# A Hymba/PEER encoder block on one core: routing look-ups and one-hot tables divided differently between VectorE and ScalarE

## The chip, the core and the metric

The kernel runs on one core of a Trainium2 chip. The metric is the device time of one execution in microseconds, as the median of several runs; the profile comes from one further execution on the same kind of core.

## The reference, cut to what matters

One encoder layer for 512 tokens of width 1024: a condition vector gives shifts, scales and gates; attention and a gating MLP share one input projection; then comes PEER, a retrieval over 128 x 128 single-neuron experts, which takes most of the time and holds the change.

```
q  = (h @ w_q) -> (tokens, 8 heads, 2 halves, 128)
s1, s2 = q[:, :, f] . keys[:, f]           # 128 scores per half
v1, i1 = top_k(s1, 16);  v2, i2 = top_k(s2, 16)
cand   = v1[:, None] + v2[None, :]         # 16 x 16
sc, ci = top_k(cand, 16)
idx    = i1[ci // 16] * 128 + i2[ci % 16]
gates  = softmax(sc)
out    = sum_k gelu(U[idx_k] . h) * gate_k * V[idx_k]
```

## The kernel before, in words

Three of the four 128-token blocks (384 tokens) go through PEER densely: for each e of 128, `dense_a` computes gelu(U_e h) for the 128 experts of row e, the result is multiplied by a table of gates and goes through V_e. The fourth block gathers its experts' rows by indirect DMA, as work inserted into the dense loop. Float32 products are made as three exact matmuls of high and low halves (`mm3`, lines 80 to 84): a cast on ScalarE makes the high half (line 77), a subtraction on VectorE the low one (line 78). So each weight tile that TensorE uses waits for one instruction of each of the two engines.

The stages around the change:

1. Query scores (lines 668 to 689): per head and half, 24 matmuls of 512 columns, a copy `qT`, four score matmuls. The weights wq have their high and low halves in two buffers each.
2. Routing on VectorE (lines 530 to 609), in two groups of four heads for the 384 dense tokens (tag d). `route_keys` takes the top 16 of 128 scores; `route_cands` adds the pairs that can be among the best 16; `route_pick` takes the top 16 of them; `route_decode` turns a candidate's number into row and column (`rcf`) and casts the key indices to bf16 (`i12f`, line 585); `route_lookup` fetches the index of each pick. A look-up compares the wanted column with 0 to 15 (line 593), multiplies by the table, which is repeated along the innermost axis (line 595), and adds up in a tree (lines 597 and 599). The one-hot tile `oh` has two buffers, one for each of the two look-ups.
3. Meanwhile TensorE computes `dense_a` for e up to 17, as far as weights and a ring of result tiles allow.
4. Table build (lines 723 to 810): the indices and gates are transposed (`gt`), then 48 steps of 8 tokens make, for each token, the one-hot of its first index times its gate (`o1`) and of its second index (`o2`), and TensorE multiplies the two into a 128 x 128 table (`gg`, line 770). Of the 8 first-index one-hots, four are made on VectorE as compare and product (line 757) and four by a bf16 compare of four tokens together (line 751) with the gate as scale on ScalarE (line 764). All eight second-index one-hots are one f32 compare (line 753). ScalarE drains the tables (line 779). Twelve further dense tiles are spread over the 48 steps. The order of TensorE, ScalarE and VectorE in this stage is that of the program.
5. Expert loop (lines 888 to 927): `dense_a(e + 30)`, the V product of e, and from the list `fill` (lines 864 to 879) the routing of the last 128 tokens (tag g) and the 256 gathers, spaced by an estimate of cost for each entry.

Outside stage 4 the order of the instructions on each engine is planned when the program is built: an instruction goes as soon as, by the planner's own estimates, its operands are ready, earlier program lines first. Each engine then works strictly in that order.

Of the kernel before, what the change touches and what calls it, by code (L numbers as in the profile page):

```python
# [19 lines left out]
P = 128  # L20
# [6 lines left out]
K = 16  # L27
# [11 lines left out]
UT = 8  # L39
# [18 lines left out]
def tile_kernel(ctx: ExitStack, tc: tile.TileContext, a: dict, out: bass.AP):  # L58
    nc = tc.nc
    ctx.enter_context(nc.allow_low_precision("float32 products as sums of exact float32r parts"))  # L60

    def pool(st, name, side=None, space=None):
        kw = {} if space is None else {"space": space}
        return st.enter_context(tc.tile_pool(name=name, bufs=1, side=side, reuse_waits="tile", **kw))
# [23 lines left out]
    iota = const("iota_s", [P, P], a["iota"])  # L88
# [29 lines left out]
    with ExitStack() as fr:  # L118
# [120 lines left out]
        for b in range(NB):  # L239
            t = B.tile([P, D], F32, name=f"x{b}", tag=f"y{b}")  # L240
# [19 lines left out]
        with ExitStack() as s1st:  # L260
# [55 lines left out]
            for b in range(NB):  # L316
                p = pss[b]
# [225 lines left out]
    def route_keys(r, b, h, f, sv):  # L543
        tmp = r["pl"].tile([P, P], F32, name=f"tmp{r['tag']}{b}{h}{f}", tag="tmp", bufs=2)
        top16(r["v12"][:, b, h, f, :], r["i12"][:, b, h, f, :], sv, tmp)

    def route_cands(r):
        n = r["nb"] * r["nh"]
        v = r["v12"].rearrange("p b h f k -> p (b h) f k")
        cand = r["pl"].tile([P, n, NC], F32, name=f"cd{r['tag']}", tag="cand", bufs=1)  # L550
        for r0, nr, ncol, p0 in STAIR:
            sh = [P, n, nr, ncol]
            nc.vector.tensor_tensor(
                cand[:, :, p0:p0 + nr * ncol].rearrange("p b (i j) -> p b i j", j=ncol),
                v[:, :, 0, r0:r0 + nr].unsqueeze(3).to_broadcast(sh),
                v[:, :, 1, :ncol].unsqueeze(2).to_broadcast(sh), op=ALU.add)
        r["cand"] = cand
        r["ci"] = r["pl"].tile([P, n, K], U32, name=f"ci{r['tag']}", tag="ci", bufs=1)
# [6 lines left out]
    def route_decode(r):  # L565
        pl, tag, ci = r["pl"], r["tag"], r["ci"]
        n = r["nb"] * r["nh"]
        rt_ = lambda m, dt=F32: pl.tile([P, n, K], dt, name=f"{m}{tag}", tag=m, bufs=1)
        t3, t2 = rt_("t3", U32), rt_("t2", U32)
        nc.vector.tensor_single_scalar(t3, ci, 3, op=ALU.logical_shift_right)  # L570
        nc.vector.tensor_single_scalar(t2, ci, 2, op=ALU.logical_shift_right)
        row, st, u = rt_("row"), rt_("rst"), rt_("ru")
        rcf = pl.tile([P, 2, n, K], BF16, name=f"rcf{tag}", tag="rcf", bufs=1)
        nc.vector.scalar_tensor_tensor(row, t3, 5.0, t2, op0=ALU.add, op1=ALU.max)
        nc.vector.scalar_tensor_tensor(row, row, 42.0, ci, op0=ALU.add, op1=ALU.max)
        nc.vector.tensor_scalar(row, row, -48.0, 0.0, op0=ALU.add, op1=ALU.max)
        nc.vector.tensor_copy(rcf[:, 0], row)
        nc.vector.tensor_scalar(st, row, 7.0, 8.0, op0=ALU.mult, op1=ALU.add)
        nc.vector.tensor_scalar(u, row, 3.0, 24.0, op0=ALU.mult, op1=ALU.add)
        nc.vector.scalar_tensor_tensor(st, row, 15.0, st, op0=ALU.mult, op1=ALU.min)  # L580
        nc.vector.scalar_tensor_tensor(st, u, 48.0, st, op0=ALU.min, op1=ALU.min)
        nc.vector.tensor_add(st, st, row)
        nc.vector.tensor_sub(rcf[:, 1], ci, st)
        i12f = pl.tile([P, n, 2, K], BF16, name=f"i12f{tag}", tag="i12f", bufs=1)
        nc.vector.tensor_copy(i12f, r["i12"].rearrange("p b h f k -> p (b h) f k"))
        r["rcf"], r["i12f"] = rcf, i12f

    def route_lookup(r, f, dst):

        n = r["nb"] * r["nh"]  # L590
        sh = [P, n, K, K]
        oh = r["pl"].tile(sh, BF16, name=f"oh{r['tag']}{f}", tag="oh", bufs=2)
        nc.vector.tensor_tensor(oh, r["rcf"][:, f].unsqueeze(2).to_broadcast(sh),
                                jrep.unsqueeze(1).to_broadcast(sh), op=ALU.is_equal)
        nc.vector.tensor_tensor(oh, oh, r["i12f"][:, :, f, :].unsqueeze(3).to_broadcast(sh), op=ALU.mult)
        for w in (8, 4, 2):
            nc.vector.tensor_add(oh[:, :, :w, :], oh[:, :, :w, :], oh[:, :, w:2 * w, :])
        o5 = oh.rearrange("p (b h) j k -> p b h j k", h=r["nh"])
        nc.vector.tensor_add(dst, o5[:, :, :, 0, :], o5[:, :, :, 1, :])
# [13 lines left out]
    with ExitStack() as qs:  # L613
# [80 lines left out]
        r = None  # L694
        for h in range(PH):
            if h + 1 < PH:
                score(h + 1)
            while ahead < FIRST + h + 1 + (LATE if h == PH - 1 else 0):
                dense_a(ahead)
                ahead += 1  # L700
            s_sb = scores.pop(h)
            hl = h % HG
            if hl == 0:
                r = route_tiles(R, f"d{h}", ND, HG)
            for b in range(ND):
                for f in range(2):
                    route_keys(r, b, hl, f, s_sb[:, b, f, :])
            if hl == HG - 1:
                hs = slice(h - HG + 1, h + 1)
                route_cands(r)  # L710
                for b in range(ND):
                    for i in range(HG):
                        route_pick(r, b, i, sca[:, b, h - HG + 1 + i, :])
                route_decode(r)
                for f, dst in ((0, i1a), (1, i2a)):
                    route_lookup(r, f, dst[:, :, hs, :])
        route_gates(R, sca, gts, ND * PH)

    flat = lambda t, b: t.rearrange("p b h k -> p b (h k)")[:, b, :]
# [3 lines left out]
    with ExitStack() as gs:  # L723
        psq = pool(gs, "psg", space=PSUM)
        G = pool(gs, "gbuild")
        tTs = []
        for b in range(ND):
            p = psq.tile([P, 512], F32, name=f"gt{b}", tag="q", bufs=6)
            for i, src in enumerate((i1a, i2a, gts)):
                nc.tensor.transpose(p[:, i * P:(i + 1) * P], flat(src, b), ident)  # L730
            tT = G.tile([P, 3, P], F32, name=f"gT{b}")
            nc.scalar.copy(tT, p[:, :384].rearrange("p (i t) -> p i t", t=P))
            tB = G.tile([P, P], BF16, name=f"gB{b}")
            nc.scalar.copy(tB, p[:, :P])  # L734
            tTs.append((tT, tB))
        HT = UT // 2
        erep = G.tile([P, P, HT], BF16, name="erep")
        nc.vector.tensor_copy(erep, iota.unsqueeze(2).to_broadcast([P, P, HT]))
        NG = TD // UT
        GPS = TC // UT  # L740
        o1s, o1b, o2s, pgs, stages = {}, {}, {}, {}, {}

        def tok(n):
            return tTs[n * UT // P], n * UT % P

        def g_eq(n):
            (tT, tB), t0 = tok(n)
            o1b[n] = G.tile([P, P, HT], BF16, name=f"o1b{n}", tag="o1b", bufs=2)
            o2s[n] = G.tile([P, UT, P], F32, name=f"o2_{n}", tag="o2", bufs=2)
            o1s[n] = G.tile([P, UT, P], F32, name=f"o1_{n}", tag="o1", bufs=2)  # L750
            nc.vector.tensor_tensor(o1b[n], erep, tB[:, t0:t0 + HT].unsqueeze(1).to_broadcast([P, P, HT]),  # L751
                                    op=ALU.is_equal)
            nc.vector.tensor_tensor(o2s[n], iota.unsqueeze(1).to_broadcast([P, UT, P]),  # L753
                                    tT[:, 1, t0:t0 + UT].unsqueeze(2).to_broadcast([P, UT, P]), op=ALU.is_equal)
            for i in range(HT, UT):
                t = t0 + i
                nc.vector.tensor_scalar(o1s[n][:, i, :], iota, tT[:, 0, t:t + 1], tT[:, 2, t:t + 1],  # L757
                                        op0=ALU.is_equal, op1=ALU.mult)

        def g_gate(n):  # L760
            (tT, tB), t0 = tok(n)
            e = o1b.pop(n)
            for i in range(HT):
                nc.scalar.activation(o1s[n][:, i, :], e[:, :, i], AF.Copy, scale=tT[:, 2, t0 + i:t0 + i + 1])  # L764

        def g_mm(n):
            o1, o2 = o1s.pop(n), o2s.pop(n)
# [50 lines left out]
    st = {}  # L818
# [46 lines left out]
    for h in range(PH):  # L865
        for f in range(2):
            fill.append((1.6, lambda h=h, f=f: route_keys(st["r"], 0, h, f, st["sg"][:, 2 * h + f, :])))
    fill.append((1.2, lambda: route_cands(st["r"])))
    for h in range(PH):
        fill.append((1.3, lambda h=h: route_pick(st["r"], 0, h, st["sc"][:, 0, h, :])))  # L870
    fill.append((4.0, lambda: route_decode(st["r"])))
    for f in range(2):
        fill.append((5.0, lambda f=f: route_lookup(st["r"], f, st["i"][f])))
    fill.append((1.2, lambda: route_gates(st["R"], st["sc"], gtg, PH)))
    fill.append((0.3, gb_idx))
    for n in range(NS):
# [138 lines left out]
```

## Time and profile before

| | |
|---|---|
| median of 3 runs | 1567.47 us (1567.18 to 1567.62) |
| the profiled execution | 1570.06 us |
| its span, first to last instruction | 1568.3 us |
| TensorE (PE) busy | 1492.6 us, 95% |
| VectorE (DVE) busy | 1240.9 us, 79% |
| ScalarE (ACT) busy | 636.6 us, 41% |
| mean granted TensorE clock | 0.981 of full speed |

Busy shares are means over stages with different limits. Durations of matmuls are modelled to their end and overlap, so starts are compared with starts. A number in square brackets at the end of a timeline row is the engine's idle time before that instruction, with what ended it. [...] In the view of busy time by stretch, a row has the stretch, its length, the busy time and number of instructions of PE, PEld (weight loads), DVE, ACT and POOL, then the granted clock, the DMA share and GB/s. In the groups by form, a row ends with the busy time in all, the mean duration of one in ns, and the idle time before them.

### The profile page before, as it was taken

To read this page: it belongs to the slowest core of one execution; us is meant where nothing else is said; L and a number is where in the kernel's file an instruction comes from. 1 tells how busy PE (TensorE), PEld (TensorE's weight loads), DVE (VectorE), ACT (ScalarE), POOL (GpSimd) and SP (SyncE) were. 2 spreads that over 40 slices of the span, in tenths; PEclk is the share of its full clock that TensorE was granted. 3 is DMA by queue.
4 is the path that set the end of the run, shared out by engine and by line. 5 is a ranking of instruction groups with operands and counts; after the bars stand their busy time and mean duration, and the time that the engine had idled before them with its cause. 6 is when DMAs were issued, how large, how long until landed. Compare 5 with 4: busy or idle time off the path is not lost.

```text
span 1568.3 us, 21451 instructions
## 1 busy us (share of the span) xinstructions
PE 1492.6 (95%) x7675; PEld 1317.9 (84%) x7675; DVE 1240.9 (79%) x2388; ACT 636.6 (41%) x1092; POOL 397.1 (25%) x335
## 2 busy tenths in 40 slices
PE   2899999998979999999999999999999999999996
PEld 1765787887879999999999999999999999998884
DVE  6937865579989997987887878878888888886774
ACT  2533434432338997334333333333333333332343
POOL 1202100000000000002554444444544544542210
PEclk9899999999999999999999999999999999999998
DMA  9626334331325769666999999988999998987873
GB/s 366 232 79 223 130 132 148 112 104 48 101 94 159 237 211 300 218 224 220 354 351 319 321 330 328 326 318 318 336 330 314 326 325 315 333 287 230 256 237 121
DMA packets 147226, 380.71 MB, mean 243 GB/s; under 512 B 11184, under 2 KB 59840, under 8 KB 146864
## 3 DMA queue, kind: packets, MB, share of 16 engines
q1 hardware_dynamic: 103472, 221.02, 40.5%
q0 software_dynamic: 42352, 153.62, 28.7%
q10 hardware_dynamic: 1296, 4.72, 0.8%
q8 instruction: 60, 0.98, 0.2%
q14 instruction: 46, 0.38, 0.1%
HBM read 349.16 MB, written 30.15 MB: 242 GB/s over the span
## 4 chain that ended last, share of the span: by engine, by line
PE 86%; DVE 7%; DMA 3%; ACT 1%; issue 1%; POOL 0%; SPq 0%; ACTq 0%; POOLq 0%; DVEq 0%
PE out L83 11%; PE out L84 11%; PE out L82 11%; PE pa L82 11%; PE pa L84 11%; PE pa L83 11%; PE gg L770 5%; DMA wada<-w_ada 2%; PE q L82 1%; PE q L84 1%; PE q L83 1%; PE yo L82 1%; PE yo L84 1%; PE yo L83 1%; DVE macc L149 1%
## 5 line engine op out<-in xcount | busy, mean ns | idle before, releaser
L842 POOL DMA_INDIRECT gu<-peer_u,idx x128 | 181.3, 1417 | 653.6 <-DVE w17l L78 467.6
L842 POOL DMA_INDIRECT gv<-peer_v,idx x128 | 173.0, 1351 | 235.0 <-DVE accg L862 209.0
L850 DVE SCALAR_TENSOR_TENSOR scr<-gu,h2g 128x1024 bf16<-128x1024 f32 x128 | 156.5, 1222 | 24.1 <-DMA gu<-peer_u,idx 21.8
L862 DVE SCALAR_TENSOR_TENSOR accg<-gv,wg,accg 128x1024 f32<-128x1024 f32 x127 | 162.8, 1282 | 7.1 <-DMA gv<-peer_v,idx 4.6
L770 PE MATMUL gg<-o,o 128*128 128x128 f32 x768 | 96.0, 280 | 3.6 <-ACT o L764 2.0
L770 PEld LDWEIGHTS gg<-o,o 128*128 128x128 f32 x768 | 94.6, 196 | 4.1 <-ACT o L764 4.1
L908 DVE TENSOR_TENSOR a<-a,g 128x384 f32<-128x384 f32 x128 | 69.1, 550 | 6.4 <-DMA g<-gd 2.9
L764 ACT ACTIVATE o<-o1b,gT 128x128 f32<-128x128 bf16 x192 | 63.4, 405 | 13.8 <-DVE o1b L751 7.2
L518 ACT ACTIVATE a<-pa 128x384 f32<-128x384 f32 x128 | 61.7, 483 | 13.2 <-PE pa L84 13.2
L149 DVE SCALAR_TENSOR_TENSOR macc<-wada,csil,macc 128x1024 f32<-128x1024 f32 x40 | 51.2, 1280 | 9.5 <-DMA wada<-w_ada 9.1
L753 DVE TENSOR_TENSOR o<-iota_s,gT 128x1024 f32<-128x1024 f32 x48 | 58.4, 1216 | 0.3 <-PE gg L770 0.2
L757 DVE TENSOR_SCALAR o<-iota_s,gT 128x128 f32<-128x128 f32 x192 | 53.2, 339 | 0.0
L779 ACT COPY st<-gg 128x512 f32<-128x512 f32 x96 | 50.5, 581 | 0.0
L159 PE MATMUL mcol<-ident_s,macc 128*128 128x128 f32 x32 | 7.4, 391 | 26.6 <-DVE macc L146 23.1
L135 POOL DMA_DIRECT2D wada<-w_ada x32 | 17.1, 535 | 59.9 <-DVE macc L149 24.3
L159 PEld LDWEIGHTS mcol<-ident_s,macc 128*128 128x128 f32 x32 | 5.5, 201 | 28.3 <-DVE macc L146 17.9
L424 ACT ACTIVATE pe<-s,mx 128x512 f32<-128x512 f32 x16 | 11.0, 688 | 28.4 <-DVE mx L422 20.8
L684 PE MATMUL sc<-keys_s,qT 128*128 128x128 f32 x128 | 18.1, 284 | 2.8 <-ACT qT L681 2.8
L751 DVE TENSOR_TENSOR o1b<-erep,gB 128x512 bf16<-128x512 bf16 x48 | 20.0, 416 | 0.9 <-ACT gB L734 0.9
L684 PEld LDWEIGHTS sc<-keys_s,qT 128*128 128x128 f32 x128 | 15.6, 191 | 5.7 <-ACT qT L681 4.3
L531 DVE MAX8 v12d<-s 128x8 f32<-128x128 f32 x48 | 12.7, 280 | 9.4 <-ACT s L686 9.4
L431 PEld LDWEIGHTS o<-vv,pts 128*128 128x128 f32 x128 | 16.1, 192 | 2.3 <-DVE mx L422 0.8
(2789 smaller groups left out, 4952.2 us busy)
## 6 DMA issues: line engine op xcount, KB each, us to landing
gd<-st SPq DMA_DIRECT2D x12, 1984.0 KB, 7.9
g<-gd SPq DMA_DIRECT2D x31, 768.0 KB, 8.4
wada<-w_ada POOLq DMA_DIRECT2D x32, 512.0 KB, 4.7
wada<-w_ada SPq DMA_DIRECT2D x16, 512.0 KB, 10.1
x<-x SPq DMA_DIRECT2D x4, 512.0 KB, 12.4
x<-x ACTq DMA_DIRECT2D x4, 512.0 KB, 3.8
x2d<-x ACTq DMA_DIRECT2D x4, 512.0 KB, 2.8
gu<-peer_u,idx POOLq DMA_INDIRECT x128, 7.3
```

The lines of the kernel that those rows point to most:

```text
L82: nc.tensor.matmul(o, lhsT=lh, rhs=rh, start=first, stop=False)
L83: nc.tensor.matmul(o, lhsT=lh, rhs=rl, start=False, stop=False)
L84: nc.tensor.matmul(o, lhsT=ll, rhs=rh, start=False, stop=last)
L149: nc.vector.scalar_tensor_tensor(acc, w, csil[:, c:c + 1], acc, op0=ALU.mult, op1=ALU.add)
L518: nc.scalar.activation(t, p[:, :TD], AF.Gelu)
L753: nc.vector.tensor_tensor(o2s[n], iota.unsqueeze(1).to_broadcast([P, UT, P]), tT[:, 1, t0:t0 + UT].unsqueeze(2).to_broadcast([P, UT, P]), ...
L764: nc.scalar.activation(o1s[n][:, i, :], e[:, :, i], AF.Copy, scale=tT[:, 2, t0 + i:t0 + i + 1])
L770: nc.tensor.matmul(pgs[n][i // 4][:, i % 4 * P:(i % 4 + 1) * P], lhsT=o2[:, i, :], rhs=o1[:, i, :], start=True, stop=True)
L842: nc.gpsimd.indirect_dma_start(out=g, out_offset=None, in_=src, in_offset=bass.IndirectOffsetOnAxis(ap=idx[:, s:s + 1], axis=0))
L850: nc.vector.scalar_tensor_tensor(scr, g, 1.0, st["h2g"], op0=ALU.mult, op1=ALU.mult, accum_out=actg[:, n:n + 1])
L862: nc.vector.scalar_tensor_tensor(accg, g, wg[:, s:s + 1], accg, op0=ALU.mult, op1=ALU.add)
L908: nc.vector.tensor_tensor(wv3, wv3, gt[:, :, e % GE, :], op=ALU.mult)
```

## The change

In the look-ups, ScalarE casts the key indices (`route_tables`) and copies each table out into a tile `rep` of the full shape (`route_rep`), so that the product on VectorE has two dense operands. `rep` and `oh` have one buffer each: the second table is spread after the first product. In the table build, both indices of four tokens are compared in one bf16 instruction of 1024 elements. ScalarE widens the second-index half to float32, and VectorE multiplies the first-index half by the gates, 512 elements at a time. Both read every eighth bf16 element in turn, since the compare leaves two indices of four tokens next to each other. The cost estimates of the inserted entries are lowered.

```
     def route_decode(r):
...
-        nc.vector.tensor_copy(i12f, r["i12"].rearrange("p b h f k -> p (b h) f k"))
-        r["rcf"], r["i12f"] = rcf, i12f
+        r["rcf"] = rcf
+
+    def route_tables(r):
+        pl, tag = r["pl"], r["tag"]
+        n = r["nb"] * r["nh"]
         i12f = pl.tile([P, n, 2, K], BF16, name=f"i12f{tag}", tag="i12f", bufs=1)
+        nc.scalar.copy(i12f, r["i12"].rearrange("p b h f k -> p (b h) f k"))
+        r["i12f"] = i12f
+        r["rep"] = {}
+
+    def route_rep(r, f):
+        n = r["nb"] * r["nh"]
+        t = r["pl"].tile([P, n, K, K], BF16, name=f"rep{r['tag']}{f}", tag="rep", bufs=1)
+        nc.scalar.copy(t, r["i12f"][:, :, f, :].unsqueeze(3).to_broadcast([P, n, K, K]))
+        r["rep"][f] = t

     def route_lookup(r, f, dst):
...
-        oh = r["pl"].tile(sh, BF16, name=f"oh{r['tag']}{f}", tag="oh", bufs=2)
+        oh = r["pl"].tile(sh, BF16, name=f"oh{r['tag']}{f}", tag="oh", bufs=1)
...
-        nc.vector.tensor_tensor(oh, oh, r["i12f"][:, :, f, :].unsqueeze(3).to_broadcast(sh), op=ALU.mult)
+        nc.vector.tensor_tensor(oh, oh, r["rep"].pop(f), op=ALU.mult)
...
             if hl == HG - 1:
                 hs = slice(h - HG + 1, h + 1)
+                route_tables(r)
+                route_rep(r, 0)
                 route_cands(r)
...
                 route_decode(r)
-                for f, dst in ((0, i1a), (1, i2a)):
-                    route_lookup(r, f, dst[:, :, hs, :])
+                route_lookup(r, 0, i1a[:, :, hs, :])
+                route_rep(r, 1)
+                route_lookup(r, 1, i2a[:, :, hs, :])
...
-            tT = G.tile([P, 3, P], F32, name=f"gT{b}")
-            nc.scalar.copy(tT, p[:, :384].rearrange("p (i t) -> p i t", t=P))
-            tB = G.tile([P, P], BF16, name=f"gB{b}")
-            nc.scalar.copy(tB, p[:, :P])
+            gT = G.tile([P, P], F32, name=f"gT{b}")
+            nc.scalar.copy(gT, p[:, 2 * P:3 * P])
+            iB = G.tile([P, P // HT, 2, HT], BF16, name=f"iB{b}")
+            nc.scalar.copy(iB, p[:, :2 * P].rearrange("p (i u k) -> p u i k", i=2, k=HT))
...
-        erep = G.tile([P, P, HT], BF16, name="erep")
-        nc.vector.tensor_copy(erep, iota.unsqueeze(2).to_broadcast([P, P, HT]))
+        erep = G.tile([P, P, 2 * HT], BF16, name="erep")
+        nc.vector.tensor_copy(erep, iota.unsqueeze(2).to_broadcast([P, P, 2 * HT]))
...
         def g_eq(n):
...
-            nc.vector.tensor_tensor(o1b[n], erep, tB[:, t0:t0 + HT].unsqueeze(1).to_broadcast([P, P, HT]),
-                                    op=ALU.is_equal)
-            nc.vector.tensor_tensor(o2s[n], iota.unsqueeze(1).to_broadcast([P, UT, P]),
-                                    tT[:, 1, t0:t0 + UT].unsqueeze(2).to_broadcast([P, UT, P]), op=ALU.is_equal)
-            for i in range(HT, UT):
-                t = t0 + i
-                nc.vector.tensor_scalar(o1s[n][:, i, :], iota, tT[:, 0, t:t + 1], tT[:, 2, t:t + 1],
-                                        op0=ALU.is_equal, op1=ALU.mult)
+            for i in range(UT // HT):
+                ohb[n, i] = G.tile([P, P, 2, HT], BF16, name=f"oh{n}_{i}", tag="ohb", bufs=2)
+                nc.vector.tensor_tensor(
+                    ohb[n, i].rearrange("p e i k -> p e (i k)"), erep,
+                    iB[:, t0 // HT + i].rearrange("p i k -> p (i k)").unsqueeze(1).to_broadcast([P, P, 2 * HT]),
+                    op=ALU.is_equal)

         def g_gate(n):
...
-            e = o1b.pop(n)
-            for i in range(HT):
-                nc.scalar.activation(o1s[n][:, i, :], e[:, :, i], AF.Copy, scale=tT[:, 2, t0 + i:t0 + i + 1])
+            for i in range(UT // HT):
+                e = ohb.pop((n, i)).rearrange("p e i k -> p i k e")
+                ts = slice(i * HT, (i + 1) * HT)
+                nc.scalar.copy(o2s[n][:, ts, :], e[:, 1])
+                nc.vector.tensor_tensor(
+                    o1s[n][:, ts, :], e[:, 0],
+                    gT[:, t0 + i * HT:t0 + (i + 1) * HT].unsqueeze(2).to_broadcast([P, HT, P]), op=ALU.mult)
...
+    fill.append((0.0, lambda: (route_tables(st["r"]), route_rep(st["r"], 0))))
     fill.append((1.2, lambda: route_cands(st["r"])))
...
-    fill.append((4.0, lambda: route_decode(st["r"])))
-    for f in range(2):
-        fill.append((5.0, lambda f=f: route_lookup(st["r"], f, st["i"][f])))
+    fill.append((3.6, lambda: route_decode(st["r"])))
+    fill.append((4.0, lambda: route_lookup(st["r"], 0, st["i"][0])))
+    fill.append((0.0, lambda: route_rep(st["r"], 1)))
+    fill.append((4.0, lambda: route_lookup(st["r"], 1, st["i"][1])))
```

## Rows read from the trace of the kernel before

**Rows 1.** Busy time by stretch, columns as told above
```profile
345.00:420.00 75.00, 68.37 (x339) 57.63 (x339) 69.93 (x351) 21.19 (x40) 0.00 (x0) 0.98 0.22 70
475.00:1536.00 1061.00, 1061.00 (x5618) 969.37 (x5618) 874.13 (x1381) 451.48 (x771) 354.88 (x257) 1.00 0.84 290
500.00:560.00 60.00, 60.00 (x466) 60.00 (x465) 58.66 (x133) 55.02 (x142) 0.00 (x0) 1.00 0.76 229
```
**Rows 2.** Timeline, first group's look-ups: start us, us, engine, line, operation
```profile
382.62 1.21 DVE L78 TENSOR_TENSOR wq12l<-wq12r,wq12h 128x1024 fp32r<-128x1024 f32 x1
...
383.88 0.50 PE L84 MATMUL q<-h2T,wq12l 128*128 128x512 f32 x1 [2.79 <-DVE wq12l L78]
```

**Rows 3.** Timeline, tail of the routing and first steps of the table build
```profile
449.01 1.22 DVE L78 TENSOR_TENSOR u15l<-u15r,u15h 128x1024 fp32r<-128x1024 f32 x1
...
450.28 0.69 PE L84 MATMUL pa<-h2T,u15l 128*128 128x384 f32 x1 [3.22 <-DVE u15l L78]
...
456.97 1.05 ACT L77 CAST u17h<-u17r 128x1024 fp32r<-128x1024 f32 x1 [10.58 <-PE pa L83]
...
458.05 1.23 DVE L78 TENSOR_TENSOR u17l<-u17r,u17h 128x1024 fp32r<-128x1024 f32 x1 [2.88 <-ACT u17h L77]
...
465.95 0.33 PE L730 MATMUL gt<-ident_s,i2a 128*128 128x128 f32 x1 [0.54 <-DVE i2a L599]
...
467.10 0.42 DVE L751 TENSOR_TENSOR o1b<-erep,gB 128x512 bf16<-128x512 bf16 x1 [0.88 <-ACT gB L734]
```

**Rows 4.** Busy time by stretch, columns as in rows 1, after the two long waits
```profile
384.00:388.00 4.00, 4.00 (x11) 3.16 (x12) 4.00 (x19) 0.00 (x0) 0.00 (x0) 0.58 0.39 135
388.00:390.00 2.00, 2.00 (x10) 1.59 (x10) 2.00 (x15) 0.00 (x0) 0.00 (x0) 0.99 0.00 0
450.00:456.00 6.00, 5.72 (x18) 5.72 (x19) 5.17 (x8) 0.00 (x0) 0.00 (x0) 0.50 0.54 175
458.00:460.00 2.00, 2.00 (x13) 2.00 (x13) 1.95 (x3) 0.41 (x2) 0.00 (x0) 1.00 0.00 0
```

**Rows 5.** Groups by form on VectorE, 345 to 475 us: busy us, mean ns | idle
```profile
L595 DVE TENSOR_TENSOR ohd<-ohd,i12fd 128x3072 bf16<-128x3072 bf16 x4 | 13.4, 3348 | 0.0
L593 DVE TENSOR_TENSOR ohd<-rcfd,jrep 128x3072 bf16<-128x3072 bf16 x4 | 7.0, 1748 | 0.0
...
L597 DVE TENSOR_TENSOR ohd<-ohd 128x1536 bf16<-128x1536 bf16 x4 | 3.8, 946 | 0.0
...
L585 DVE CAST i12fd<-i12d 128x384 bf16<-128x384 uint32 x2 | 0.7, 352 | 0.0
```

**Rows 6.** Groups by form on ScalarE, whole span, copies of 512 and 2048 elements
```profile
L779 ACT COPY st<-gg 128x512 f32<-128x512 f32 x96 | 50.5, 581 | 0.0
...
L351 ACT COPY vv<-v 128x512 f32<-128x512 f32 x4 | 2.3, 586 | 1.1 <-PE v L350 1.1
...
L77 ACT CAST wl0h<-wl0r 128x2048 fp32r<-128x2048 f32 x1 | 1.9, 1899 | 11.5 <-DMA wl0r<-w_in 11.5
```

**Rows 7.** Chain that ended last, in the table build: start us, us, what
```profile
537.58 1.78 PE gg L770 x16
...
540.41 1.78 PE gg L770 x16
```

**Rows 8.** Timeline of the table build, one step of VectorE, and ScalarE beside it
```profile
522.62 0.42 DVE L751 TENSOR_TENSOR o1b<-erep,gB 128x512 bf16<-128x512 bf16 x1
522.96 1.22 DVE L753 TENSOR_TENSOR o<-iota_s,gT 128x1024 f32<-128x1024 f32 x1
...
523.14 1.32 ACT L764 ACTIVATE o<-o1b,gT 128x128 f32<-128x128 bf16 x4 [0.19 <-DVE o1b L751]
...
524.10 1.11 DVE L757 TENSOR_SCALAR o<-iota_s,gT 128x128 f32<-128x128 f32 x4
...
524.73 1.05 ACT L779 COPY st<-gg 128x512 f32<-128x512 f32 x2
525.12 0.42 DVE L751 TENSOR_TENSOR o1b<-erep,gB 128x512 bf16<-128x512 bf16 x1
```

More of the change, by code (lines that the diff above doesn't have):

```diff
@@ L725, in tile_kernel @@
         G = pool(gs, "gbuild")
+        HT = UT // 2
         tTs = []
@@ L730, in tile_kernel @@
                 nc.tensor.transpose(p[:, i * P:(i + 1) * P], flat(src, b), ident)
-            tT = G.tile([P, 3, P], F32, name=f"gT{b}")
-            nc.scalar.copy(tT, p[:, :384].rearrange("p (i t) -> p i t", t=P))
-            tB = G.tile([P, P], BF16, name=f"gB{b}")
-            nc.scalar.copy(tB, p[:, :P])
-            tTs.append((tT, tB))
-        HT = UT // 2
-        erep = G.tile([P, P, HT], BF16, name="erep")
-        nc.vector.tensor_copy(erep, iota.unsqueeze(2).to_broadcast([P, P, HT]))
+            gT = G.tile([P, P], F32, name=f"gT{b}")
+            nc.scalar.copy(gT, p[:, 2 * P:3 * P])
+            iB = G.tile([P, P // HT, 2, HT], BF16, name=f"iB{b}")
+            nc.scalar.copy(iB, p[:, :2 * P].rearrange("p (i u k) -> p u i k", i=2, k=HT))
+            tTs.append((gT, iB))
+        erep = G.tile([P, P, 2 * HT], BF16, name="erep")
+        nc.vector.tensor_copy(erep, iota.unsqueeze(2).to_broadcast([P, P, 2 * HT]))
         NG = TD // UT
         GPS = TC // UT
-        o1s, o1b, o2s, pgs, stages = {}, {}, {}, {}, {}
+        ohb, o1s, o2s, pgs, stages = {}, {}, {}, {}, {}
         def tok(n):
@@ L746, in g_eq @@
         def g_eq(n):
-            (tT, tB), t0 = tok(n)
-            o1b[n] = G.tile([P, P, HT], BF16, name=f"o1b{n}", tag="o1b", bufs=2)
+            (gT, iB), t0 = tok(n)
             o2s[n] = G.tile([P, UT, P], F32, name=f"o2_{n}", tag="o2", bufs=2)
             o1s[n] = G.tile([P, UT, P], F32, name=f"o1_{n}", tag="o1", bufs=2)
-            nc.vector.tensor_tensor(o1b[n], erep, tB[:, t0:t0 + HT].unsqueeze(1).to_broadcast([P, P, HT]),
-                                    op=ALU.is_equal)
-            nc.vector.tensor_tensor(o2s[n], iota.unsqueeze(1).to_broadcast([P, UT, P]),
-                                    tT[:, 1, t0:t0 + UT].unsqueeze(2).to_broadcast([P, UT, P]), op=ALU.is_equal)
-            for i in range(HT, UT):
-                t = t0 + i
-                nc.vector.tensor_scalar(o1s[n][:, i, :], iota, tT[:, 0, t:t + 1], tT[:, 2, t:t + 1],
-                                        op0=ALU.is_equal, op1=ALU.mult)
-        def g_gate(n):
-            (tT, tB), t0 = tok(n)
-            e = o1b.pop(n)
-            for i in range(HT):
-                nc.scalar.activation(o1s[n][:, i, :], e[:, :, i], AF.Copy, scale=tT[:, 2, t0 + i:t0 + i + 1])
+            for i in range(UT // HT):
[4 more added lines that the diff above has]
+                    op=ALU.is_equal)
+        def g_gate(n):
+            (gT, iB), t0 = tok(n)
+            for i in range(UT // HT):
[5 more added lines that the diff above has]
+                    gT[:, t0 + i * HT:t0 + (i + 1) * HT].unsqueeze(2).to_broadcast([P, HT, P]), op=ALU.mult)
         def g_mm(n):
```

## The prediction

> **What bounds the kernel now.** I read the stretches first, then the waits inside the one that has idle time. From 475 us to 1536 us TensorE is busy for all of 1061.00 us while VectorE has 874.13 and ScalarE 451.48 [rows 1]: no saving on another engine shortens this part, and whatever is gained before 475 us is carried to the end one for one. From 345 to 420 us, where the first four heads are routed, TensorE has 68.37 of 75 us and VectorE 69.93: there two engines hand the bound to each other.
>
> The waits say where. At 383.88 us TensorE resumes after 2.79 us without wq12l, the low half of a query weight; VectorE made it only at 382.62, behind the first two look-ups [rows 2]. In the tail of routing the same happens at 450.28: 3.22 us for u15l, made at 449.01 behind a product of 3.35 us [rows 3, 5]. That delays ScalarE's cast u17h to 456.97 and with it VectorE, idle for 2.88 us at 458.05. i2a, the end of the chain, is waited for a last 0.54 us by the transposes at 465.95. [...]
>
> **The change, part by part.** *Look-ups.* A product of 3072 elements takes 3348 ns where the table is repeated along the innermost axis; the compare of equal size takes 1748 [rows 5]. The change hands the product two dense bf16 operands, as the first tree addition has: 946 ns for 1536. On the line through 946 and 1748, 3072 elements cost 1.75 us, so each product saves 1.60. Ends: 1.75, or 3.35 if the table was not the cause. I take 1.75, as compare and addition lie on one line. The cast of the indices (352 ns alone, about 0.27 in a run of instructions) leaves VectorE too. Per group of four heads: 2 x 1.60 + 0.27 = 3.47 us of VectorE.
>
> ScalarE gets the cast (some 0.5) and two spreads of 3072 elements per group. Its copies take 581 ns for 512 and 1899 for 2048 [rows 6], so 0.858 ns each and 2.78 us a spread. Spread 0 waits for the last key index; candidates and 12 picks lie between that and its use, and ScalarE's casts queue behind it. Spread 1 can start only when product 0 has left the single buffer, and product 1 waits for it. Between them VectorE has four additions and the next compare, some 0.9 + 0.5 + 0.3 + 0.3 + 1.7 = 3.7 us, which hides 2.78 if ScalarE is free within 0.9 us. In the tail it is: it waits 10.58 us for TensorE there [rows 3]. One one-hot buffer in place of two costs no wait between engines, since all its users are on VectorE, but dependent instructions follow each other with less between them: 0 to 0.5 us per group.
>
> *First group, heads 0 to 3.* wq12l comes 3.2 to 3.5 us earlier than at 382.62, more than the 2.79 that TensorE waited: the wait goes, and with it, I take it, the half clock, 4.0 - 11 x 0.2 = 1.8 by the slices, 1.5 if 11 is rounded up. I take 2.8 + 1.5 = **4.3 us**. Ends: 0 (a ScalarE wait takes the place of this one) and 4.6.
>
> *Tail, heads 4 to 7.* u15l is behind one cast and one product: 0.27 + 1.60 = 1.87 us earlier, so 1.35 of the 3.22 stays. If so short a wait leaves the clock up, 18 matmuls at 2/13 us take 2.8 instead of 5.7: 2.9 saved, taken as 2.6. TensorE then reaches the transposes 1.9 + 2.6 = 4.5 us earlier. VectorE's chain shortens by 3.47 and the idle 2.88 (u17h follows TensorE), less 0.5: 5.9 earlier. The later one decides: **4.5 us**. Ends: 1.9 (half clock as before) and 5.9. What is late next is the last dense tile on TensorE. erep doubles to 1024 elements, 0.3 us more; the first compare waits 0.88 us for ScalarE at that point [rows 3], so it costs nothing, and 0.3 if that wait shrinks.
>
> *Table build, 48 steps of 8 tokens.* The TensorE pieces of 16 start 2.83 us apart [rows 7]. VectorE's cycle was 525.12 - 522.62 = 2.50: compare 0.34, f32 compare 1.14, four gated compares 1.02 [rows 8]. Over 500 to 560 us it is busy 58.66 of 60 and ScalarE 55.02 [rows 1], by 21.1 steps 2.78 and 2.61 a step. Now there are two bf16 compares of 1024 elements (0.34 + 512 x 0.52 ns = 0.60 each) and two products of 512 on VectorE, and two widening copies of 512 on ScalarE in place of four gates (1.32). No row has a product that reads bf16 at a distance of 8 elements. Ends: 0.61, the f32 compare's rate (1.14 for 1024), and 1.02, the four gated compares of together 512. For the copy: 0.52, half of the pair at 524.73 [rows 8], and 1.32, the four gates. I take the lower ends, since both new instructions are single long ones, and since ScalarE drains PSUM with neighbours 512 bytes apart in 581 ns, against 586 for an adjacent 512 [rows 6]. VectorE: 2.78 - 2.50 + 1.20 + 1.22 = 2.70; ScalarE: 2.61 - 1.32 + 1.05 = 2.34. Both stay under 2.83: **0 us** saved, as TensorE covers both. At the upper ends VectorE needs 3.52 and ScalarE 3.93, and the cover is gone. With two one-hot buffers of 4 tokens, the compares of a step wait for copy and product of the step before; TensorE runs one step behind with two buffers of results, so this is hidden while both engines are under 2.83. The ramp of the first three steps: -1 to +1.
>
> [...]
>
> *Last 128 tokens, inside the expert loop.* Two products get shorter and two spreads of 2048 elements (1.90 by the cast of that size) and a cast go to ScalarE; the estimates that space the inserted work fall by 2.4. All lies after 475 us, under a TensorE that never pauses, with ScalarE busy 451 of 1061 us [rows 1]: 0; up to 2 us if a spread waiting for VectorE holds the casts behind it longer than their lead. No DMA moves to another queue.
>
> **Sum.** 4.3 + 4.5 = 8.8 us. The profiled execution took 1570.06 (span 1568.3 and 1.76 around it), so 1561.3 by it; it lies 2.59 above the median of the runs, 1567.47, so the median becomes **1558.7**. Own range of this case: 1553 (both upper ends, 1 us of ramp, a little reordering) to 1565. A measurement of this kernel tells 0.2%, 3.1 us, from no change.
>
> **Rivals.**
> 1. *The build becomes bound by VectorE (slower).* Place: product and widening copy, where neighbouring elements lie 16 bytes apart. It decides as soon as a product or a copy takes more than about 0.67 us from start to start. If each element takes two slots, the product costs 2 x 0.57 = 1.14 and the copy 0.95: VectorE 2.78 - 2.50 + 1.20 + 2.28 = 3.76 a step, ScalarE 3.19. Then 48 x 0.93 = 44.6 us come on top: 1558.7 + 44.6 = 1603; at half that surcharge 1577. For: the upper ends above, and a margin of only 0.13 us a step. Against: no strided row is slow. [...] Chance 0.32.
> 2. *The tables come late (no change).* ScalarE works in order; if spread 1 stands behind a cast that waits for TensorE, as u17h does, product 1 waits and the look-ups gain nothing. At 2.78 for what saves 1.60, a spread on the path is a loss of 1.18; in both groups that is 2.36, against 2 x 1.87 = 3.74 that the first products and the casts still save: 1.4 us are left, 1566. Against: the order is planned by readiness and spread 1 is ready before u17h. Chance 0.10.
> 3. *The product does not get faster.* Then only the casts leave VectorE: 2 x 0.27, 1567. Against: the addition's row. Chance 0.03.
>
> **How the numbers follow.** The forecast has 0.55. Faster: 0.55 and the better fifth of rival 2, 0.57; slower: rival 1 and the worst of rival 2, 0.33; the same: 0.10. The range must hold rival 1 in part, or it would leave out three in ten: 1553 to 1605, with some 0.1 beyond both ends.
>
> **What would show it.** The product of 3072 at about 1750 ns and the spreads at 2.8 us beside picks; no wait of TensorE for wq12l; a wait under 1.5 us for u15l; the pieces of 16 still 2.83 us apart. Wrong: products of 512 at 1.2 us with TensorE idle in every step; product 1 waiting for the spread; new waits of TensorE for casts; or an order of VectorE's work that puts other halves behind the look-ups.

## The result, and the profile after

The changed kernel takes **1601.66 us** (median of 5 runs, 1601.43 to 1604.28); the kernel before, run beside it, 1567.62 (1567.18 to 1569.22). The ratio is 1.0219, with a 95% interval of 1.0205 to 1.0233: 2.2% slower, where 1558.7 was forecast. That is the time of the first rival, 1603. The profiled execution has a span of 1599.8 us.

Busy time by stretch of the changed kernel (stretch, its length, then PE, PEld, DVE, ACT and POOL busy with their instructions, granted clock, DMA share, GB/s), to be read against [rows 1]:

```profile
345.00:420.00 75.00, 69.81 (x350) 60.03 (x349) 68.20 (x359) 27.58 (x42) 0.00 (x0) 0.98 0.23 75
500.00:560.00 60.00, 52.73 (x366) 49.24 (x365) 56.60 (x70) 55.87 (x78) 0.00 (x0) 0.96 0.57 176
700.00:1560.00 860.00, 860.00 (x4256) 774.85 (x4255) 689.20 (x906) 306.53 (x423) 354.75 (x257) 1.00 0.86 305
```

In the table build TensorE has lost its full stretch: 52.73 of 60 us where it had 60.00. Behind the build it has no gap again, so the expert loop, with the look-ups of the last 128 tokens in it, pays and gains nothing. The loss is the build's alone, and its length shows it. This row groups the 768 build products of the changed kernel, with shortest, median and longest duration in ns and then the first and the last start:

```profile
L787 PE MATMUL gg<-o,o x768: 270/275/554, 462.3 to 639.1; 128*128 128x128 f32 x192
```

The same row of the kernel before has 468.8 to 607.2. The build lasts 176.8 us in place of 138.4: **+38.4**. It starts 6.5 us earlier, but some 2.5 of that the profile of before had lost ahead of the change: the cast wq9h, which the change does not touch, starts at 342.9 there and at 340.4 after. The routing gained about **4**. Together +34.4; the medians differ by 34.0.

The groups of the changed kernel by form, from 480 to 600 us and, for the two look-up lines, over the whole span (busy us, mean ns, idle before):

```profile
L778 ACT CAST o<-oh 128x512 f32<-128x512 bf16 x66 | 70.8, 1125 | 9.3 <-DVE oh L768 9.3
...
L779 DVE TENSOR_TENSOR o<-oh,gT 128x512 f32<-128x512 bf16 x65 | 67.2, 1078 | 0.0
...
L768 DVE TENSOR_TENSOR oh<-erep,iB 128x1024 bf16<-128x1024 bf16 x66 | 42.5, 689 | 0.0
L796 ACT COPY st<-gg 128x512 f32<-128x512 f32 x64 | 34.4, 595 | 0.0
...
L598 ACT COPY repd<-i12fd 128x3072 bf16<-128x3072 bf16 x4 | 11.0, 2752 | 5.6 <-DVE ohd L608 5.6
...
L608 DVE TENSOR_TENSOR ohd<-ohd,repd 128x3072 bf16<-128x3072 bf16 x4 | 7.0, 1748 | 0.0
```

The look-up's product went from 3348 ns [rows 5] to 1748, as forecast, and a spread takes 2752 (2.78 forecast). But the widening copy of 512 takes 1125 ns and the build's product of 512 takes 1078, while the copy out of PSUM of as many elements, 512 bytes apart, takes 595, little more than the 581 of [rows 6]. These are durations of single instructions. From start to start, which is how the prediction priced them, a pair of copies takes 2.01 to 2.05 us and a pair of products 1.95 to 1.99, as here, where the compare behind a pair starts 1.95 us after it:

```profile
525.03 2.04 DVE L779 TENSOR_TENSOR o<-oh,gT 128x512 f32<-128x512 bf16 x2
526.98 1.28 DVE L768 TENSOR_TENSOR oh<-erep,iB 128x1024 bf16<-128x1024 bf16 x2
```

One period of four steps on the chain of waits of the changed kernel (start, us, what), against the pieces of 16 that stood there before [rows 7]:

```profile
524.62 2.11 ACT o L778 x2
526.73 0.98 ACT st L796 x2
...
527.93 2.14 ACT o L778 x2
...
530.94 2.14 ACT o L778 x2
...
534.31 2.15 ACT o L778 x2
536.46 0.95 ACT u23h L77
...
537.44 1.23 DVE u23l L78
538.67 0.61 DVE oh L768
...
539.38 2.11 ACT o L778 x2
```

The chain no longer runs through TensorE. It is ScalarE, copy after copy, and once in four steps a detour: the cast u23h stands in ScalarE's order, VectorE's low half u23l follows it, the next compare stands behind u23l, and the copy of that step waits for the compare. 539.38 - 524.62 = 14.76 us for four steps, 3.69 a step; TensorE needs 2.83.

### The profile page after: what moved, and what is told of

Same layout as the page of the kernel before. It is cut to its first block, busy times and chain, and to the rows that moved or that the text cites. A ratio compares the mean times of both kernels' runs of the same rounds, so it can differ in the third digit from the quotient of the medians.

```text
span 1599.8 us, 21357 instructions
## 1 busy us (share of the span) xinstructions
PE 1504.6 (94%) x7675; PEld 1320.4 (83%) x7675; DVE 1266.9 (79%) x2289; ACT 690.6 (43%) x1005; POOL 396.6 (25%) x335
## 4 chain that ended last, share of the span: by engine, by line
PE 75%; ACT 9%; DVE 9%; DMA 3%; issue 2%; POOL 0%; SPq 0%; ACTq 0%; POOLq 0%; DVEq 0%
PE out L84 11%; PE out L83 11%; PE out L82 11%; PE pa L84 10%; PE pa L82 10%; PE pa L83 10%; ACT o L778 6%; DMA wada<-w_ada 2%; ACT st L796 2%; PE q L82 1%; PE q L83 1%; PE q L84 1%; PE yo L82 1%; PE yo L83 1%; PE yo L84 1%
## 5 line engine op out<-in xcount | busy, mean ns | idle before, releaser
L787 PE MATMUL gg<-o,o 128*128 128x128 f32 x768 | 105.4, 292 | 25.6 <-DVE o L779 25.4
L787 PEld LDWEIGHTS gg<-o,o 128*128 128x128 f32 x768 | 98.3, 201 | 36.2 <-ACT o L778 33.2
L778 ACT CAST o<-oh 128x512 f32<-128x512 bf16 x96 | 103.2, 1128 | 14.4 <-DVE oh L768 14.2
L779 DVE TENSOR_TENSOR o<-oh,gT 128x512 f32<-128x512 bf16 x96 | 99.3, 1078 | 0.0
L768 DVE TENSOR_TENSOR oh<-erep,iB 128x1024 bf16<-128x1024 bf16 x96 | 62.0, 689 | 2.5 <-ACT iB L751 2.3
L418 PE MATMUL s<-kr,qr 64*128 64x512 f32 x32 | 18.0, 641 | 0.0
```

Of the source, the lines that this page charges most:

```text
L778: nc.scalar.copy(o2s[n][:, ts, :], e[:, 1])
L779: nc.vector.tensor_tensor(o1s[n][:, ts, :], e[:, 0], gT[:, t0 + i * HT:t0 + (i + 1) * HT].unsqueeze(2).to_broadcast([P, HT, P]), op=ALU.mult)
L787: nc.tensor.matmul(pgs[n][i // 4][:, i % 4 * P:(i % 4 + 1) * P], lhsT=o2[:, i, :], rhs=o1[:, i, :], start=True, stop=True)
```

## The experiments

The first four ran on one chip (before: 1568.54, 10 runs), the next four on another (1567.82, 10 runs), the last on a third (1569.67, 9 runs). Three theories of the slow build were open: the **step** (16 bytes between neighbours makes an instruction slow), the **types** (reading bf16 and writing f32), and the **shared tile** (two engines reading one tile disturb each other).

**1. The look-ups alone.** The new routing with the table build of before.

> The kernel before with the look-ups of the change alone; the table build is that of before. Theory S (the loss is all in the build, from bf16 elements read 16 bytes apart): this part is a gain. In the trace of the changed kernel the last score copy before the tail came 3.4 us earlier and the first piece of the build 6.5 us earlier than in the trace of before, but 2.5 us of that was already there at 340 us, ahead of the change; so 1 us from the first group and some 3 from the tail: 1563.5 us, 1562 to 1565. Rival L (part of the loss is in the look-ups, hidden by a luckier start): 1566 to 1570. The prediction on record had 1558.7 for this part.

Measured: 1562.53 us (1560.66 to 1564.32), ratio 0.9964 (0.9950 to 0.9977). The look-ups gain, but about 6 us by the medians and not the 8.8 of the forecast. The waits of TensorE in the routing of this kernel, from 345 to 475 us (total us, times, longest):

```profile
PE pa L84 <- DVE u8l L78: 4.2, 1, 4.2
...
PE pa L84 <- DVE u15l L78: 1.8, 1, 1.8
```

The wait for wq12l [rows 2] is gone, and one of 4.2 us for u8l, the low half of a dense tile, is new. It is in the changed kernel too, where ScalarE's cast u8h starts at 358.0 us and VectorE makes u8l only at 393.14, behind key work; the timeline there, and the clock behind it and behind u15l (columns as in the first fence):

```profile
393.14 1.22 DVE L78 TENSOR_TENSOR u8l<-u8r,u8h 128x1024 fp32r<-128x1024 f32 x1
...
394.41 0.45 PE L84 MATMUL pa<-h2T,u8l 128*128 128x384 f32 x1 [4.24 <-DVE u8l L78]
```

```profile
396.00:398.00 2.00, 2.00 (x9) 1.81 (x8) 1.38 (x10) 0.65 (x2) 0.00 (x0) 0.50 0.57 221
446.00:450.00 4.00, 4.00 (x16) 4.00 (x15) 4.00 (x11) 0.70 (x1) 0.00 (x0) 0.57 0.76 249
```

**2. The build alone.** The routing of before with the new table build.

> The kernel before with the table build of the change alone; the look-ups are those of before. Theory S: the 48 steps take 176.8 us from the first to the last piece instead of 138.4, so 38 us on top of 1567.6: 1606 us, 1604 to 1608. Rival (the two parts help or hurt each other, e.g. ScalarE's spreads delay the build): this plus the look-ups alone would not add up to the changed kernel's 1601.7.

Measured: 1605.04 us (1603.68 to 1605.43), ratio 1.0231 (1.0216 to 1.0247). The build costs 36.5 us, the look-ups give 6.0: 30.5 together, where the full change cost 34.0 in its own comparison; the intervals, some 2 us to either side of each, allow that difference. In the profiles the parts add closely: this build lasts 176.4 us (176.8 in the full change) and starts at 466.0 us behind the old routing, 3.7 us later than behind the new one (4.3, if counted from the cast wq9h, which starts at 339.8 here and at 340.4 there).

**3. The same data, 8 bytes apart.** The whole change, with the one-hot tile laid out by list first, so that one list's neighbours are 4 elements apart instead of 8. Types, engines, counts and the shared tile stay. The constant operand of the compare is half as long and is read twice; the compare takes 682 ns in place of 689, so that plays no part.

```diff
-G.tile([P, P, 2, HT], BF16, name=f"oh{n}_{i}", tag="ohb", bufs=2)
+G.tile([P, 2, P, HT], BF16, name=f"oh{n}_{i}", tag="ohb", bufs=2)
...
-e = ohb.pop((n, i)).rearrange("p e i k -> p i k e")
+e = ohb.pop((n, i)).rearrange("p i e k -> p i k e")
```

> The changed kernel with the one-hots of four tokens laid out index by index, so that product and widening copy read every fourth bf16 element (8 bytes apart) in place of every eighth (16 bytes). Theory S (a new 16-byte stretch with every element costs a second slot): the product falls from 1078 to about 690 ns, the copy from 1128 to about 610, the pieces of 16 stand 2.84 us apart again, and the time is that of the look-ups alone, 1563.5 us (1561 to 1566). Rival M (it is the mixture of bf16 and f32 operands that is slow, not the distance): both stay at 1.1 us, the time at 1601. Rival C (VectorE and ScalarE disturb each other in the one tile that both read): the same, 1595 to 1602.

Measured: 1562.62 us (1560.09 to 1564.97), ratio 0.9957 (0.9944 to 0.9971): faster than before. Its groups by form from 480 to 600 us:

```profile
L779 DVE TENSOR_TENSOR o<-oh,gT 128x512 f32<-128x512 bf16 x86 | 55.2, 682 | 0.0
L768 DVE TENSOR_TENSOR oh<-erep,iB 128x1024 bf16<-128x1024 bf16 x84 | 54.0, 682 | 0.0
L778 ACT CAST o<-oh 128x512 f32<-128x512 bf16 x85 | 53.0, 673 | 11.5 <-DVE oh L768 10.3
```

and its pieces on TensorE's timeline:

```profile
521.24 1.95 PE L787 MATMUL gg<-o,o 128*128 128x128 f32 x16
524.08 1.95 PE L787 MATMUL gg<-o,o 128*128 128x128 f32 x16
```

The product falls from 1078 to 682 ns, the copy from 1125 to 673, and the pieces are 2.84 us apart again: the cover is back. Types and shared tile are as before, so neither can be what made the instructions slow; the step is left. The build now gains nothing against that of before (this run and experiment 1 have the same time), which is the 0 us that the forecast gave it.

**4. The price of the step.** Behind the last output of the kernel before, 96 added instructions, four of each kind: a product on VectorE and a copy on ScalarE of 512 elements, at steps from 2 to 32 bytes, bf16 and f32, the step in what is read or in what is written. Its time (1609.82, one run) says nothing.

```diff
+ph = lambda t, s: t[:, :P * s].rearrange("p (e s) -> p s e", s=s)[:, :4]
...
+for _ in range(4): nc.vector.tensor_tensor(o3(od), ph(pb, 8), gb, op=ALU.mult)
+for _ in range(4): nc.scalar.copy(o3(oa), ph(pb, 8))
```

> The kernel before with instructions added after its outputs: products with a gate and copies, each of 512 elements, four times, from bf16 at 2, 4, 8, 16 and 32 bytes from element to element and from f32 at 4, 8, 16 and 32 bytes, and writes of f32 at 8, 16 and 32 bytes. Theory S: 0.69 us on VectorE and 0.61 on ScalarE up to 8 bytes; 1.08 and 1.13 from 16 bytes on, for f32 as for bf16, and no more at 32. If it grows with the distance, 32 bytes cost more than 16; if it counts elements and not bytes, f32 at 32 bytes (8 elements) is the first slow one. Rival M: all bf16 cases are slow and no f32 case is. Writes: no theory has a number from a row; 0.69 if only reads are concerned. The time itself says nothing, some 60 us longer.

The groups by form of the added stretch: bf16 read from adjacent elements (line 969 on VectorE, 970 on ScalarE), at 8, 16 and 32 bytes (973, 975, 977 on VectorE; 974, 976 on ScalarE), f32 read at 16 (983), f32 written at 8 and 16 (987, 989):

```profile
L969 DVE TENSOR_TENSOR od<-pb,pg 128x512 f32<-128x512 bf16 x4 | 2.8, 688 | 0.1
...
L970 ACT CAST oa<-pb 128x512 f32<-128x512 bf16 x4 | 2.5, 618 | 0.1
...
L973 DVE TENSOR_TENSOR od<-pb,pg 128x512 f32<-128x512 bf16 x4 | 2.8, 692 | 0.1
...
L975 DVE TENSOR_TENSOR od<-pb,pg 128x512 f32<-128x512 bf16 x4 | 4.2, 1060 | 0.1
...
L977 DVE TENSOR_TENSOR od<-pb,pg 128x512 f32<-128x512 bf16 x4 | 4.3, 1074 | 0.1
...
L974 ACT CAST oa<-pb 128x512 f32<-128x512 bf16 x4 | 2.6, 656 | 0.1
...
L976 ACT CAST oa<-pb 128x512 f32<-128x512 bf16 x4 | 4.4, 1100 | 0.1
...
L983 DVE TENSOR_TENSOR od<-pf,pg 128x512 f32<-128x512 f32 x4 | 4.3, 1068 | 0.1
...
L987 DVE TENSOR_TENSOR od<-pf,pg 128x512 f32<-128x512 f32 x4 | 2.8, 692 | 0.1
...
L989 DVE TENSOR_TENSOR od<-pf,pg 128x512 f32<-128x512 f32 x4 | 4.3, 1073 | 0.1
```

Up to 8 bytes a product costs 692 ns at most; at 16 it costs 1060 and at 32 hardly more. A copy costs 618 ns adjacent, 656 at 8 bytes and 1100 at 16. It counts in bytes: f32 pays at the same 16, which for it is 4 elements (1068 ns; at 8, two elements, 691). Distances between 8 and 16 bytes were not run. VectorE and ScalarE read the same tile beside each other here in the fast cases as in the slow ones, and all other work of the kernel is done by then.

**5 and 6. Which engine binds the build?** Only one of the two stretched instructions reads 512 adjacent elements, first ScalarE's copy, then VectorE's product.

```diff
+c = a.rearrange("p e i k -> p (e i k)")[:, :HT * P].rearrange("p (t e) -> p t e", e=P)
...
-nc.scalar.copy(o2s[n][:, ts, :], e[:, 1])
+nc.scalar.copy(o2s[n][:, ts, :], c)
```

> The changed kernel with ScalarE's widening copy reading 512 adjacent elements of the one-hot tile instead of every eighth; the right second one-hots are left out, the work is the same in number and size. VectorE's product keeps its step of 16 bytes. It asks which of the two stretched instructions binds the build. If VectorE binds (two compares of 0.6 and two products of 1.02 from start to start, and 0.28 of other work: 3.5 us a step): the copy falls to about 0.6 us, the pieces of 16 stay 3.4 to 3.6 us apart, 1588 to 1597 us. If ScalarE bound it, or only both together do: pieces 2.8 to 3.0 apart, 1560 to 1570 us. If the copy is slow for another reason than its step: copy still above 1.0 us, 1601.

> The mirror of it: VectorE's product reads 512 adjacent elements (the right first one-hots are left out), ScalarE's copy keeps its step of 16 bytes. ScalarE then has two copies of 1.07 and two score copies of together 0.98 and some 0.2 of other work, 3.3 us a step, VectorE 2.7. If both engines are over TensorE's 2.84 by themselves: pieces 3.2 to 3.4 apart, 1579 to 1590 us. If only VectorE is: 2.84 apart, 1562 us.

Measured: copy adjacent 1591.05 us (1589.12 to 1592.77), ratio 1.0152 (1.0136 to 1.0167); product adjacent 1600.89 (1599.74 to 1601.56), ratio 1.0210 (1.0194 to 1.0226). Pieces that follow a wait on TensorE's timeline, one in four steps, with the copy adjacent:

```profile
507.50 2.12 PE L789 MATMUL gg<-o,o 128*128 128x128 f32 x16 [1.14 <-DVE o L781]
...
521.35 2.13 PE L789 MATMUL gg<-o,o 128*128 128x128 f32 x16 [1.12 <-DVE o L781]
```

with the product adjacent:

```profile
510.63 2.11 PE L789 MATMUL gg<-o,o 128*128 128x128 f32 x16 [1.56 <-ACT o L780]
...
525.40 2.11 PE L789 MATMUL gg<-o,o 128*128 128x128 f32 x16 [1.90 <-ACT o L780]
```

VectorE with its slow product alone sets (521.35 - 507.50) / 4 = 3.46 us a step; ScalarE with its slow copy alone sets 14.77 / 4 = 3.69, the pace of the full change. So **the chain over ScalarE binds**, and VectorE would be a bound of its own right under it. ScalarE's own work is no longer than VectorE's: of the 14.76 us of the period shown above, 0.99 is its wait for the compare, and 13.77 / 4 = 3.44. What lifts the chain over VectorE's 3.46 is the detour, once in four steps, over the cast, VectorE's low half and the compare behind it. Mending the product alone buys nothing that can be told, mending the copy alone about 11 us, both the whole. My expectation for the second run, 1579 to 1590, was too low: it counted ScalarE's work, 3.3 us a step, and left out the wait of 0.25 (0.99 in four steps) for the compare behind the dense tile's low half, and priced ScalarE's other work too low.

**7. The missing gain of the first group.** Experiment 3 with each dense tile's split issued ahead of the next score.

```diff
+hl = a_load(ahead)
 if h + 1 < PH:
     score(h + 1)
...
-    dense_a(ahead)
+    dense_a(ahead, hl)
```

> The version with reads 8 bytes apart, and in the routing loop the split of each dense tile (the cast and the low half) is issued before the score of the next head instead of behind it. Theory: what the first group's look-ups saved was lost because u8l, the low half of the next dense tile, stands behind key work in VectorE's order; issued earlier it is ready, the wait of 4.2 us for u8l and the half clock behind it go, and the time falls from 1562.6 by 3 to 5 us, to 1557 to 1560. Rival: VectorE is full there (67.5 of 75 us from 345 to 420), so whatever half stands last is late and another wait takes its place: 1561 to 1565.

Measured: 1560.76 us (1560.14 to 1564.58), ratio 0.9955 (0.9942 to 0.9969), as experiment 3 (0.9957). Among the waits of TensorE the one for u8l is there with 4.3 us.

The edit did not move what it was to move: the order of VectorE's work is planned by readiness, and u8l stands where it stood. It tells nothing on the theory.

**8. The low halves on GpSimd.** Experiment 3, the subtractions of the routing loop's dense tiles moved off VectorE (in the tail too; there are 11 in the stretch from 339 to 455 us, not the 15 that I had counted).

```diff
-dense_a(ahead)
+dense_a(ahead, a_load(ahead, nc.gpsimd))
```

> The version with reads 8 bytes apart, and the low halves of the dense tiles in the routing loop made by GpSimd, which stands idle there, instead of VectorE. That takes 15 subtractions of 1.13 us, about 17 us, off VectorE between 340 and 475 us. Theory (VectorE's order and load make the late halves): the waits for u8l, u15l, u12l and u14l of together 7.4 us and the half clock behind them go: 1552 to 1557. Rival: GpSimd's subtraction is too long (over about 6 us, a tile's share of the stretch), or slows VectorE beside it: new waits of TensorE for the same halves, 1561 or above.

Measured: 1562.98 us (1561.73 to 1565.00), ratio 0.9968 (0.9956 to 0.9980): nothing gained over experiment 3. The stretch of the first group and the waits of TensorE:

```profile
345.00:420.00 75.00, 73.94 (x384) 64.36 (x383) 69.37 (x360) 31.04 (x48) 9.41 (x4) 1.00 0.23 73
```

```profile
PE pa L82 <- ACT u16h L77: 4.2, 1, 4.2
...
PE pa L84 <- POOL u16l L78: 2.2, 1, 2.2
```

The wait for u8l is gone and TensorE has 73.94 of 75 us, where the changed kernel has 69.81. But the edit costs something ahead of that stretch: the subtractions u2l to u4l now stand before the load of the keys in GpSimd's order, which issues it at 284.3 us (261.1 in experiment 3), and TensorE waits 1.4 us for it. From GpSimd's last small instruction ahead of the scores (line 114, 260.11 us; 260.59 in experiment 3) to the last copy qT (410.2; 413.3) this kernel is 2.6 us quicker than experiment 3, and from there to the build 3.2 slower: the tail takes it all back. There the spread of the second table waits 4.85 us on ScalarE for VectorE's first product, and the casts u16h and u17h queue behind it; and VectorE's product beside GpSimd's subtractions takes 3.71 us, in the changed kernel 1.75:

```profile
443.27 2.75 ACT L598 COPY repd<-i12fd 128x3072 bf16<-128x3072 bf16 x1 [4.85 <-DVE ohd L608]
...
446.31 1.03 ACT L77 CAST u16h<-u16r 128x1024 fp32r<-128x1024 f32 x1
```

```profile
447.42 3.17 POOL L78 TENSOR_TENSOR u16l<-u16r,u16h 128x1024 fp32r<-128x1024 f32 x1 [8.34 <-ACT u16h L77]
450.55 3.88 POOL L78 TENSOR_TENSOR u17l<-u17r,u17h 128x1024 fp32r<-128x1024 f32 x1
```

```profile
448.49 3.71 DVE L608 TENSOR_TENSOR ohd<-ohd,repd 128x3072 bf16<-128x3072 bf16 x1
```

**9. The low halves on GpSimd, the tail's back on VectorE.** Experiment 8, with `nc.gpsimd` only for h under 7.

> As the run with GpSimd's low halves, but the last nine dense tiles, those of the tail behind head 7, have theirs on VectorE again. In that run the first stretch gained (TensorE busy 73.9 of 75 us from 345 to 420, against 69.8) and the tail gave it back: TensorE waited 4.2 us for the cast u16h, queued on ScalarE behind a spread that waited for VectorE, and 2.2 us for GpSimd's u16l, while VectorE's product took 3.71 us beside GpSimd's subtraction in place of 1.75. Theory (those are what gave it back, and the wait for u8l was what the first group had lost): the first stretch keeps its 4 us, the tail is as in the version with reads 8 bytes apart (u15l waited for 1.8 us), 1557 to 1560 us. Rival (the tail ends when VectorE's and ScalarE's order lets it, whatever was gained before): another wait in the tail takes the gain, 1561 to 1564.

Measured: **1557.45 us** (1556.79 to 1560.82), ratio 0.9932 (0.9919 to 0.9946), the best of all. The first group's stretch and, of the tail, the 4 us from 446; then the waits left in the routing, and the build products:

```profile
345.00:420.00 75.00, 73.93 (x383) 64.37 (x383) 72.20 (x364) 30.26 (x48) 2.41 (x1) 1.00 0.25 80
...
446.00:450.00 4.00, 4.00 (x25) 4.00 (x24) 3.93 (x7) 1.32 (x2) 0.00 (x0) 1.00 0.42 131
```

```profile
PE gt L747 <- DVE i2a L612: 3.7, 1, 3.7
...
PE pa L84 <- DVE u15l L78: 0.5, 1, 0.5
```

```profile
L787 PE MATMUL gg<-o,o x768: 270/275/551, 457.6 to 595.0; 128*128 128x128 f32 x192
```

The build starts at 457.6 us, in the changed kernel at 462.3. Of the seven subtractions that moved, only u8l lies in the first group's stretch, and there the wait for u8l and the half clock behind it are gone (1.00 over the stretch): that is what the first group had lost. The other six and the planner's new order shift work ahead of 345 us as well, and the keys come late as in experiment 8 (1.4 us), so this is no clean measure of that one wait. Counted as there (line 114 at 259.95, last qT at 409.2), experiment 9 is 3.4 us quicker than experiment 3 to the last copy qT and 2.7 from there to the build. The tail gained too, which I had not expected: TensorE waits 0.5 us for u15l in place of 1.8, and the clock from 446 to 450 us is 1.00, with 25 matmuls, where the changed kernel has 0.57 and 16. The tail now ends with VectorE's chain, the forecast's other candidate for that end: the transposes wait 3.7 us for i2a.

## Why the prediction was wrong

**The step that failed** is the table build's "I take the lower ends, since both new instructions are single long ones, and since ScalarE drains PSUM with neighbours 512 bytes apart in 581 ns". The product was taken at 0.61 us and takes 0.98 to 1.00 from start to start; the copy at 0.52 and takes 1.02. Both lie inside the ends of the text, the product at its upper one. With the measured values (1.97 and 2.04 a pair) the text's own sums give 2.78 - 2.50 + 1.20 + 1.97 = 3.45 us a step for VectorE, as experiment 5 has it, and 2.61 - 1.32 + 2.04 = 3.33 for ScalarE: both over TensorE's 2.83, and the cover is gone. What misled was the row chosen as nearest: the PSUM copy has a large step, but it reads another memory, and experiment 4 shows that a step of 16 or 32 bytes in SBUF costs what that row does not pay (a copy of 512 takes 1100 and 1116 ns). The old gates read at 8 bytes, where such a copy takes 656 ns against 618 adjacent, so they could not show it. "Against: no strided row is slow" was true of the rows and no evidence.

The text said itself: "No row has a product that reads bf16 at a distance of 8 elements", and gave the first rival 0.32; with a margin of 0.13 us a step in the forecast, an untested price should have weighed more. Experiment 4 has that price: a product of 512 takes 692 ns at 8 bytes and 1060 at 16, and it goes by bytes, not elements (f32 at 16 bytes, 1068).

**The first rival** had the place and the 16 bytes, and its time (1603) came out within 2 us, but not by its own terms; so near is in part luck. No run shows its two slots for each element: at 16 bytes a product costs 1.53 times, and a copy 1.68 times, what it costs at 8 (experiment 4). It priced VectorE at 3.76 us a step and ScalarE at 3.19, and named VectorE. Experiments 5 and 6 show VectorE at 3.46 and the chain over ScalarE at 3.69. It put 44.6 us for the build on top of a routing gain of 8.8; 38.4 and about 4 came, and the two errors nearly cancel. ScalarE's terms over four steps of the changed kernel are four pairs of copies 8.14, eight copies out of PSUM (line 796) 4.10, other work 1.53 and the wait 0.99, 14.76 in sum. The copy was low by 0.07 each; ScalarE's other work came to (4.10 + 1.53) / 4 = 1.41 in place of 1.29; the wait was not foreseen. Two side figures of this rival were off as well: by its own sums a copy decides only above 0.77 us, (2.83 - 2.34 + 1.05) / 2, and not at 0.67, and half of the 44.6 us gives 1581, not 1577.

**Look-ups.** The product (1748 ns) and the spread (2752) came out as worked out. No VectorE product waited for a spread, so the second rival did not happen in this change. What the prediction feared only for the last tokens, a spread that waits for VectorE and holds the casts behind it, showed in experiment 8's tail.

**First group, 4.3 us: about 1 came.** wq12l came early enough, as forecast. But the text listed "an order of VectorE's work that puts other halves behind the look-ups" as what could go wrong, and nearly that happened: u8l stood behind the key work of the next heads, TensorE waited 4.24 us, and the granted clock behind that is 0.50 from 396 to 398 us, where behind the wait for wq12l it was 0.58 ([rows 4], where the forecast's 11 matmuls stand too). Experiment 9, which takes u8l off VectorE, has neither that wait nor the low clock in this stretch (1.00).

**Tail, 4.5 us: about 3 came.** The wait for u15l shrank to 1.78 us (1.35 forecast), but the assumption that "so short a wait leaves the clock up" (its 18 matmuls and 2/13 us are from [rows 4]) failed: at 446 to 450 us the granted clock is 0.57. The rest was right: VectorE's idle time before u17l, 2.88 us before, is 0.37, and the transposes then wait for the last dense tile on TensorE.

**Last tokens and erep, 0 us:** right. TensorE is busy 860.00 of 860 us from 700 on, and the doubled erep is hidden behind the wait for the transposed indices.

## What to carry to other kernels

Price an instruction by the bytes between its neighbours in SBUF: here 8 cost VectorE next to nothing and ScalarE 6%, and 16 cost 53% and 68% more than 8, so two lists interleaved in one tile can double the step for both readers, and swapping two axes of that tile was worth about 39 us. Where an engine is covered by a margin of a tenth of a microsecond a step, measure the one instruction whose price no row shows before building on it. Where an engine makes a late operand earlier, look for the next one in its order before counting the gain: here the wait moved from wq12l to u8l and kept its clock loss (0.50 from 396 to 398 us).

## What the runs showed that I had not expected

- A step costs the same in what is **written**: f32 written at 8 bytes 692 ns, at 16 bytes 1073.
- From 16 to 32 bytes the price hardly moves: 1060 and 1074 ns for the product, 1100 and 1116 for the copy.
- VectorE beside GpSimd: the look-up's product took 3.71 us beside GpSimd's subtraction, and 1.75 alone. A subtraction of 1024 elements takes GpSimd 2.38 to 2.59 us in the other places from 300 us on, and 3.17 and 3.88 in that one. GpSimd's u16l ends at 450.59, and the product at 452.20, 1.61 us later; no run here shows why both took longer.
